# First MLP of a two-layer trunk: up-projection operands formed from unnormalised h, each token's factor applied at the relu, and seven products for all sixteen up quads

## The chip, the cores and the metric

The kernel runs on one core of a Trainium2 chip. The time is that of one execution on the device, in microseconds (us), from several runs; the lower the better. One more execution was taken with the hardware profiler, and all rows below are from it. Engines: PE is TensorE (matmuls; PEld is its weight load), DVE is VectorE, ACT is ScalarE, POOL is GpSimd, and SP issues most of the DMAs.

## The reference, cut to what matters

A trunk of two layers on 1024 tokens of width 1024, all in float32. Layer 0 mixes tokens with a gated MLP, layer 1 with dilated attention. A dense MLP with a squared relu stands behind each mixer. The change touches the MLP of layer 0 and the last projection of the mixer ahead of it.

```
def _rms_norm(x, g):
    y = xf * lax.rsqrt(jnp.mean(xf * xf, axis=-1, keepdims=True) + EPS)
    return (y * g).astype(x.dtype)

for layer in range(DEPTH):                      # DEPTH = 2
    y = _rms_norm(h, mix_norm_g[layer])
    y = mixer(y)                                # layer 0: ... (u * gate) @ w_out
    h = h + y
    y = _rms_norm(h, mlp_norm_g[layer])
    h = h + jnp.square(jax.nn.relu(y @ w_up[layer])) @ w_down[layer]   # 1024 -> 4096 -> 1024
return _rms_norm(h, final_norm_g)
```

The factor of the root mean square is one positive number per token, so relu((r * z) @ w) = r * relu(z @ w), with z = h * g and r the token's factor.

## The kernel before, in words

**Layout.** h is kept transposed: eight tiles `h[m]` of 128 channels by 1024 tokens, worked on in two halves of 512 tokens, s = 0 and 1. A tile of tokens by channels that PE is to use is split in two by `split` (L226, L227): ACT writes the high part in the short float32 format that PE takes in one pass, DVE subtracts it from the source to get the low part. One product of a 128x128 weight block with a block of 128x512 is then three matmuls (high x high, high x low, low x high), issued in L198.

**Products.** The MLP's hidden width is cut in 16 quads. A quad is a 2 x 2 block product: two blocks of 128 hidden channels (i) by two token halves (s), over two halves of the input channels (j), each of 4 tiles. Done plainly that is eight block products of 12 matmuls; with Strassen-like sums of weights and operands it is seven. The seven operands of the tokens' side are called t1 to t7, each of four tiles; t1, t2 and t3 are plain blocks, t4 to t7 are differences. The seven on the weights' side are made by `Weights.steps` from four raw tiles (L382, L383, L384, L387 on GpSimd, splits on ACT and DVE), in the order 4, 1, 5, 6, 2, 7, 3, and they are used in the order 1, 5, 6, 2, 7, 3, 4. Each has a buffer of a pool of eight (`wpool`), which also holds the projection's weights.

**The projection ahead of the MLP.** The groups of output tiles are (0, 1), (2,), (3,), (4, 5, 6, 7), each for both halves. Per tile and half PE does 24 matmuls, `add_h` (L339, DVE) adds the result to h, and `Square.add` squares it on ACT (L279), and adds the squares up on GpSimd (L284), for the last tile on DVE (L288).

**Between projection and MLP.** Behind the last tile of a half, `start_terms` puts a generator on the planner `Flow`. It sums the squares with one-column matmuls, forms the inverse root (`rsqrt`, L256 to L265), spreads it over the partitions by transposes (L205), multiplies h by it (L425 for half 0, L444 for half 1), splits the product, and forms differences (L448, L449 on DVE, L450 and L451 on GpSimd). `Flow` counts the time that PE's instructions take, and lets such a generator go on when its own delay is over; that fixes PE's order at build time. The other engines' orders are made by a list scheduler that goes by program order; `tc.high_priority(offset=PRIO)` moves an instruction 60 places ahead in it. Every engine then works through its queue in order.

**The first two quads.** The differences aren't there yet when the MLP begins, so quads 0 and 1 are done together and plainly, 8 products each, with weights from `plain`: first all of half 0 in four banks, then all of half 1. Relu and square are on ACT (L849, L850), `hidden_terms` forms the operands of the down-projection (L855 to L861). Quads 2 to 4 take seven products through `opening`, which leaves time for the rest of the operands; quads 5 to 15 take the shorter path at the end of `mlp`, in which ACT copies one partial sum from bank to bank (L979) and the results are finished with adds on DVE (L1002, L1008). The second layer's MLP uses the same function.

**Pools.** `slots` has 37 buffers of one 4 KB row per partition (h, the projection's inputs `us`, the operands), `tpool` 13 buffers of half that size.

Of the kernel before, what the change touches and what calls it, by code (L numbers as in the profile page):

```python
# [19 lines left out]
P = 128  # L20
# [11 lines left out]
def half(s):  # L32
    return slice(s * HALF, (s + 1) * HALF)


def blk(b, n=1):
    return slice(b * P, (b + n) * P)
# [72 lines left out]
OPEN = 5  # L110
# [19 lines left out]
def trunk(ctx: ExitStack, tc: tile.TileContext, xT, w_u, w_v, w_o, w_s, b_s, w_qkv, w_vt, w_bo, rel,  # L130
# [63 lines left out]
    def at_bank():  # L194
        return psa.tile([P, HALF], F32, tag="at", name="at")
# [141 lines left out]
    def add_h(o, cols, ps):  # L337
        x = h[o][:, cols]
        nc.vector.tensor_tensor(x, x, ps, op=ALU.add)  # L339
# [165 lines left out]
    def start_terms(sq, s, gi, terms):  # L505
        flow.add((terms.second if s else terms.first)(sq, gi), LAT["sum"])


    wd = {(i, p): dram.tile([P, 2, HALF], F32, name=f"wd{i}_{p}", bufs=1) for i in (*sum(PREPARED, BESIDE), APART) for p in SEVEN}

# [307 lines left out]


    sq = [Square(half(0)), Square(half(1))]  # L820
    terms = Terms()
    for tiles in ((0, 1), (2,), (3,), (4, 5, 6, 7)):
        w = [weight(w_o[m]) for m in tiles]
        for s in range(2):
            for i, m in enumerate(tiles):
                b = mm_bank()
                mm(b, w[i], KCOLS, us[s])
                add_h(m, half(s), b)
                sq[s].add(m)
            if tiles[-1] == 7:  # L830
                start_terms(sq[s], s, 1, terms)
                if s == 0:
                    first = [plain(0, q) for q in range(2)]


    hidden = {}
# [7 lines left out]
        for what, t in terms.items():  # L844
            nc.sync.dma_start(hidden_tile(k, what), t)

    def squared(t, src=None):

        nc.scalar.activation(t, t if src is None else src, AF.Relu)  # L849
        nc.scalar.activation(t, t, AF.Square)  # L850

    def hidden_terms(q, c11, c21, c12, c22, t2, store=True):
# [13 lines left out]
    def mlp(layer, x, first, last, stored=None):  # L866


        def up_weights(q):
            return Weights(lambda i, j: w_up[layer, q, i, j])  # L870


        tiles = [(q, i) for q in range(2) for i in range(2)]
        c = {}

        def held_terms(q):
            hidden_terms(q, c[q, 0, 0], c[q, 1, 0], c[q, 0, 1], c[q, 1, 1], c[q, 0, 0])

        for s in range(2):
            banks = [at_bank() if (n < 2) == (s == 1) else mm_bank() for n in range(4)]  # L880
            if s == 0:
                banks = [mm_bank() if n < 3 else at_bank() for n in range(4)]
            order = [(j, k) for j in range(2) for k in range(4)] if s == 0 else [(j, k) for k in range(4) for j in range(2)]
            for n, (j, k) in enumerate(order):
                xs = x.blocks[j, s]
                flow.until(lambda: len(xs) > k)
                for b, (q, i) in zip(banks, tiles):
                    three(b, first[q][i, j], blk(k), xs[k], n == 0, n == 7)
                    flow.pump()
            for b, (q, i) in zip(banks, tiles):  # L890
                c[q, i, s] = temp()
                with tc.high_priority(offset=PRIO):
                    squared(c[q, i, s], b)
                if s and i and q == 0:
                    held_terms(q)
            if s == 0:
                w = up_weights(2)
                for _ in w.steps():
                    pass
        x.rest()  # L900

        def opening(q, w, more):

            a = mm_bank()
            product(a, w[1], x.t[1])
            if q > 2:
                more()
            u = temp()
            evacuated = nc.scalar.activation(u, a, AF.Copy).ins
            if q == 2:  # L910
                with tc.issue_after(evacuated):
                    more()
# [12 lines left out]
            if q > 2:  # L925
                more()
            nc.vector.tensor_tensor(u, u, b, op=ALU.add)
            e = at_bank()
            product(e, w[7], x.t[7])
            if q > 2:  # L930
                more()
            emptied = nc.vector.tensor_tensor(c22, c22, e, op=ALU.add).ins
            if q == 2:
                with tc.issue_after(evacuated), tc.issue_after(emptied):
                    t4()
                    more()
                    more()
                    held_terms(1)
            nc.vector.tensor_tensor(c22, c22, u, op=ALU.add)
# [12 lines left out]
            nc.vector.tensor_tensor(c21, u, e, op=ALU.add)  # L952
            squared(c21)
            return c11, c21, c12, c22

        for q in range(2, 16):
            down = Down(layer) if q == 15 else None
            wn = down.weights(0) if down else up_weights(q + 1)
            forward, calls = ahead(wn), [0]

            def more():
                forward()
                calls[0] += 1
                if q >= OPEN and calls[0] in LATER:
                    save()
                    next(coming_late[layer], None)
                if q == 15 and calls[0] == 7:
                    save()

            more()  # L970
            if q < OPEN:
                c11, c21, c12, c22 = opening(q, w, more)
            else:
                a = at_bank()
                product(a, w[1], x.t[1])
                more()
# [12 lines left out]
                product(sums, w[6], x.t[6], True)  # L989
                more()  # L990
                c12 = temp()
                with tc.high_priority(offset=PRIO):
                    nc.scalar.activation(c12, sums, AF.Copy)
                if down:
                    down.early(SEVEN[:4])
                product(a, w[2], x.t[2], True)
                more()
                c11 = temp()
                squared(c11, a)
                product(sums, w[7], x.t[7], True)  # L1000
                more()
                nc.vector.tensor_tensor(c22, c22, sums, op=ALU.add)  # L1002
                squared(c22)
                if down:
                    down.early(SEVEN[4:])
                product(d, w[3], x.t[3], True)
                more()
                nc.vector.tensor_tensor(c12, c12, d, op=ALU.add)  # L1008
# [12 lines left out]
        down.close(last, stored)  # L1021
# [935 lines left out]
```

## Time and profile before

| | us |
|---|---|
| median of 3 runs (lowest, highest) | 2108.82 (2108.45, 2113.14) |
| profiled execution | 2107.84 |
| its span, first to last instruction | 2106.1 |
| PE busy | 2083.1 |
| DVE busy | 1572.8 |
| ACT busy | 1183.3 |
| POOL busy | 498.7 |
| mean granted PE clock | 0.998 |

Busy times are shares of the span; a busy PE need not be at its peak, since matmuls overlap. In the rows of the profile "L198 PE MATMUL at<-y,wp" names line, engine, operation, output and inputs; a bracket at the end says how long the engine was idle before and what ended the wait; "x12" is a count.

### The profile page before, as it was taken

How to read it: one execution, taken by the hardware profiler on the slowest of the kernel's cores; microseconds unless marked ns; L12 is line 12 of the kernel's file. 1: busy time of each engine (PE TensorE's matmuls, PEld its weight loads, DVE VectorE, ACT ScalarE, POOL GpSimd, SP SyncE). 2: the span in 40 equal slices, each digit the busy share in tenths (PEclk: the TensorE clock that was granted, in tenths of full speed). 3: DMA queues.
4: the chain of work that ended last, by engine and by line, in shares of the span. 5: the costliest groups of instructions: out<-in, count | busy, mean ns of one | idle time of the engine just before them, and what ended most of it. 6: DMA issues, size and time to landing. Idle time of an engine off the chain costs nothing.

```text
span 2106.1 us, 30736 instructions
## 1 busy us (share of the span) xinstructions
PE 2083.1 (99%) x10160; PEld 1720.9 (82%) x10160; DVE 1572.8 (75%) x2902; ACT 1183.3 (56%) x2387; POOL 498.7 (24%) x368
## 2 busy tenths in 40 slices
PE   9999999999999999999999999999999999999998
PEld 7888888888888888888888788888888888888887
DVE  7878759766689998887746666757985446987776
ACT  7645435566675555435556666776556556544432
POOL 3000124323324333430000000002432222433244
PEclk9999999999999999999999999999999999999999
DMA  6428813688766767644865656482256443655432
GB/s 221 130 91 297 308 36 135 200 278 271 261 221 195 230 213 226 233 160 151 307 208 154 184 163 187 156 271 80 91 196 204 146 152 131 203 163 163 141 115 80
DMA packets 224756, 387.10 MB, mean 184 GB/s; under 512 B 39897, under 2 KB 67668, under 8 KB 224596
## 3 DMA queue, kind: packets, MB, share of 16 engines
q1 hardware_dynamic: 215456, 383.77, 55.4%
q10 hardware_dynamic: 9140, 1.36, 0.4%
q8 instruction: 80, 1.31, 0.3%
q14 instruction: 80, 0.66, 0.1%
HBM read 252.24 MB, written 132.81 MB: 183 GB/s over the span
## 4 chain that ended last, share of the span: by engine, by line
PE 84%; DVE 8%; DMA 2%; ACT 2%; issue 2%; POOL 1%; SPq 0%; DVEq 0%; POOLq 0%; ACTq 0%
PE mm L198 42%; PE at L198 40%; PE at L205 2%; DVE y L227 1%; DVE t L227 1%; DVE tr L227 1%; DMA t<-in_w_qkv 1%; DMA h<-in_xT 1%; DVE wp L227 0%; DVE q L1438 0%; DVE r L444 0%; DVE hx L227 0%; DMA r<-in_w_v 0%; POOL t L284 0%; DVE b L449 0%
## 5 line engine op out<-in xcount | busy, mean ns | idle before, releaser
L227 DVE TENSOR_TENSOR wp<-r,wp 128x512 fp32r<-128x512 f32 (+3 forms) x399 | 324.7, 819 | 124.4 <-ACT wp L226 122.1
L226 ACT ACTIVATE wp<-r 128x512 fp32r<-128x512 f32 (+3 forms) x399 | 236.2, 597 | 317.2 <-PE at L198 195.4
L198 PE MATMUL mm<-t,wp 128*128 128x512 f32 x1368 | 344.8, 395 | 0.0
L198 PE MATMUL at<-hx,wp 128*128 128x512 f32 x1452 | 341.0, 389 | 1.7 <-DVE h L1080 1.6
L198 PEld LDWEIGHTS at<-hx,wp 128*128 128x128 f32 x1452 | 272.1, 188 | 60.0 <-DVE h L1080 3.1
L198 PEld LDWEIGHTS mm<-t,wp 128*128 128x128 f32 x1368 | 250.7, 188 | 52.9 <-issue 0.7
L284 POOL TENSOR_TENSOR t<-t 128x512 f32<-128x512 f32 (+1 forms) x60 | 76.8, 1281 | 801.7 <-ACT t L279 799.7
L198 PE MATMUL at<-y,wp 128*128 128x512 f32 x1008 | 245.3, 389 | 0.0
L198 PE MATMUL mm<-hx,wp 128*128 128x512 f32 x984 | 234.3, 389 | 0.0
L198 PEld LDWEIGHTS at<-y,wp 128*128 128x128 f32 x1008 | 189.0, 188 | 39.6 <-issue 0.4
L198 PEld LDWEIGHTS mm<-hx,wp 128*128 128x128 f32 x984 | 184.5, 188 | 38.7 <-DVE hx L227 0.2
L198 PE MATMUL mm<-y,wp 128*128 128x512 f32 x816 | 209.8, 396 | 1.1 <-DVE y L227 0.6
L382 POOL TENSOR_TENSOR t<-r 128x512 f32<-128x512 f32 (+3 forms) x62 | 85.0, 1372 | 476.3 <-DMA r<-in_w_up 146.4
L198 PEld LDWEIGHTS mm<-y,wp 128*128 128x128 f32 x816 | 149.2, 188 | 33.0 <-DVE y L227 1.1
L227 DVE TENSOR_TENSOR hx<-t,hx 128x512 fp32r<-128x512 f32 x192 | 158.7, 831 | 6.1 <-ACT hx L226 5.6
L198 PE MATMUL mm<-y,whi 128*128 128x512 f32 x512 | 158.3, 390 | 1.1 <-DVE t L790 1.1
L198 PE MATMUL at<-t,wp 128*128 128x512 f32 x552 | 130.6, 389 | 0.0
L226 ACT ACTIVATE hx<-t 128x512 fp32r<-128x512 f32 x192 | 119.1, 628 | 19.9 <-DMA t<-hid 16.0
L384 POOL TENSOR_TENSOR r<-r 128x512 f32<-128x512 f32 (+3 forms) x62 | 90.5, 1459 | 165.4 <-DVE wp L227 151.9
L198 PEld LDWEIGHTS at<-t,wp 128*128 128x128 f32 x552 | 103.6, 188 | 21.5
L1080 DVE TENSOR_TENSOR h<-h,at 128x512 f32<-128x512 f32 x144 | 97.8, 680 | 27.6 <-PE at L198 27.1
L198 PEld LDWEIGHTS mm<-y,whi 128*128 128x128 f32 x512 | 95.5, 188 | 21.1 <-issue 1.5
(247 smaller groups left out, 3466.2 us busy)
## 6 DMA issues: line engine op xcount, KB each, us to landing
t<-hid SPq DMA_DIRECT2D x182, 256.0 KB, 4.3
wd<-tr SPq DMA_DIRECT2D x154, 256.0 KB, 3.1
wp<-wd SPq DMA_DIRECT2D x77, 512.0 KB, 4.2
hid<-t SPq DMA_DIRECT2D x140, 256.0 KB, 2.9
r<-in_w_up SPq DMA_DIRECT2D x120, 256.0 KB, 2.8
r<-in_w_dn SPq DMA_DIRECT2D x80, 256.0 KB, 2.7
hid<-b SPq DMA_DIRECT2D x56, 256.0 KB, 2.9
r<-in_w_v SPq DMA_DIRECT2D x48, 256.0 KB, 3.2
```

Source lines behind the costliest of these rows:

```text
L198: nc.tensor.matmul(out, lhsT, rhs, **kw)
L205: nc.tensor.transpose(out, src, ident)
L226: return (nc.scalar.activation(hi, src, AF.Copy).ins, (engine or nc.vector).tensor_tensor(lo, src, hi.bitcast(F32), op=ALU.subtract).ins)
L227: (engine or nc.vector).tensor_tensor(lo, src, hi.bitcast(F32), op=ALU.subtract).ins)
L284: nc.gpsimd.tensor_tensor(self.acc, self.acc, sq, op=ALU.add)
L382: tt(r3, r[0, 0], r[1, 0], op=ALU.subtract)
L384: tt(r[1, 1], r[1, 0], r[0, 0], op=ALU.subtract)
L1080: return engine.tensor_tensor(hs[i, s], hs[i, s], src, op=ALU.add).ins
```

## The change

A new class `RawTerms` takes the place of `Terms` for the first MLP. As each projected tile leaves PE, its operands are made from h times the channel's weight only (`put`): from half 0 t1 (m = 0 to 3) and t2 (m = 4 to 7); from half 1 t5 (m = 0 to 3), and for m = 4 to 7 t7, t6, t3 and t4 together. The inverse root is still formed per half (`norm`), but it is only copied to an SBUF row tile (`rows`), and multiplied in at the relu, which moves from ACT to one DVE instruction (maximum with 0, times the row). `add_h` of the projection gets priority. All sixteen quads of the first MLP then take seven products on the shorter path, starting with quad 0; the weights of quad 0 come from `Weights` in place of `plain`. The second MLP keeps its path.

```
+    class RawTerms:
+        def __init__(self, gi):
+            self.t = {p: [] for p in range(1, 8)}
+            self.g = vec[:, gi, :]
+            self.neg = ...                         # -g
+            self.rows = slot(name="rows")
+        def scaled(self, p, x, g):
+            hi, lo = pair(f"t{p}").both()
+            nc.scalar.activation(hi, x, AF.Copy, scale=g)
+            nc.vector.scalar_tensor_tensor(lo, x, g, hi.bitcast(F32), op0=ALU.mult, op1=ALU.subtract)
+            self.t[p].append(Pair((hi, lo)))
+        def put(self, m, s):
+            j, k = divmod(m, 4)
+            stt = nc.vector.scalar_tensor_tensor
+            x0, x1 = h[m][:, half(0)], h[m][:, half(1)]
+            g = self.g[:, m:m + 1]
+            if s == 0:
+                self.scaled(1 + j, x0, g)
+            elif j == 0:
+                t5 = temp()
+                nc.scalar.activation(t5, x1, AF.Copy, scale=g)
+                stt(t5, x0, self.neg[:, m:m + 1], t5, op0=ALU.mult, op1=ALU.add)
+                self.t[5].append(pair("t5").split(t5))
+            else:
+                g0, y, t = self.g[:, k:k + 1], temp(), temp()
+                nc.scalar.activation(y, h[k][:, half(1)], AF.Copy, scale=g0)
+                stt(t, x1, g, y, op0=ALU.mult, op1=ALU.subtract)
+                t7 = pair("t7").split(t)
+                stt(y, h[k][:, half(0)], g0, t, op0=ALU.mult, op1=ALU.add)
+                self.t[6].append(pair("t6").split(y))
+                self.t[7].append(t7)
+                self.scaled(3, x1, g)
+                stt(t, x0, g, y, op0=ALU.mult, op1=ALU.subtract)
+                self.t[4].append(pair("t4").split(t))
+        def norm(self, sq, s):
+            yield from sq.sums()
+            r = sq.rms()
+            yield LAT["rms"]
+            pb = spread(r)
+            with tc.high_priority(offset=PRIO):
+                nc.scalar.activation(self.rows[:, half(s)], pb, AF.Copy)
...
-    terms = Terms()
+    terms = RawTerms(1)
...
                 mm(b, w[i], KCOLS, us[s])
-                add_h(m, half(s), b)
+                with tc.high_priority(offset=PRIO):
+                    add_h(m, half(s), b)
                 sq[s].add(m)
+                terms.put(m, s)
             if tiles[-1] == 7:
-                start_terms(sq[s], s, 1, terms)
+                flow.add(terms.norm(sq[s], s), LAT["sum"])
                 if s == 0:
-                    first = [plain(0, q) for q in range(2)]
+                    first = Weights(lambda i, j: w_up[0, 0, i, j])
+                    for _ in first.steps():
+                        pass
...
-    def squared(t, src=None):
-        nc.scalar.activation(t, t if src is None else src, AF.Relu)
+    def squared(t, src=None, rows=None):
+        src = t if src is None else src
+        if rows is None:
+            nc.scalar.activation(t, src, AF.Relu)
+        else:
+            nc.vector.scalar_tensor_tensor(t, src, 0.0, rows, op0=ALU.max, op1=ALU.mult)
         nc.scalar.activation(t, t, AF.Square)
...
+        begin = 0 if rows[0] is not None else 2     # the plain start only where begin is 2
...
-        for q in range(2, 16):
+        for q in range(begin, 16):
...
-            if q < OPEN:
+            if begin and q < OPEN:
                 c11, c21, c12, c22 = opening(q, w, more)
...
-                squared(c11, a)
+                squared(c11, a, rows[0])
...
-                squared(c22)
+                squared(c22, None, rows[1])
...
-                squared(c12)
+                squared(c12, None, rows[1])
...
-                squared(c21, sums)
+                squared(c21, sums, rows[0])
```

More of the change, by code (lines that the diff above doesn't have):

```diff
@@ L506, in start_terms @@
         flow.add((terms.second if s else terms.first)(sq, gi), LAT["sum"])
+    class RawTerms:
+        def __init__(self, gi):
+            self.t = {p: [] for p in range(1, 8)}
+            self.g = vec[:, gi, :]
+            self.neg = small.tile([P, KT], F32, name="neg", bufs=1)
+            nc.vector.tensor_scalar(self.neg, self.g, -1.0, None, op0=ALU.mult)
+            self.rows = slot(name="rows")
[34 more added lines that the diff above has]
+                nc.scalar.activation(self.rows[:, half(s)], pb, AF.Copy)
     wd = {(i, p): dram.tile([P, 2, HALF], F32, name=f"wd{i}_{p}", bufs=1) for i in (*sum(PREPARED, BESIDE), APART) for p in SEVEN}
@@ L870, in up_weights @@
             return Weights(lambda i, j: w_up[layer, q, i, j])
[L873 to L886, printed above, removed]
-                for b, (q, i) in zip(banks, tiles):
[L888 to L899, printed above, removed]
@@ L900, in mlp, with held_terms @@
-        x.rest()
+        rows = [x.rows[:, half(s)] for s in range(2)] if isinstance(x, RawTerms) else [None, None]
+        begin = 0 if rows[0] is not None else 2
+        w = first
+        if begin:
+            tiles = [(q, i) for q in range(2) for i in range(2)]
+            c = {}
+            def held_terms(q):
+                hidden_terms(q, c[q, 0, 0], c[q, 1, 0], c[q, 0, 1], c[q, 1, 1], c[q, 0, 0])
+            for s in range(2):
+                banks = [at_bank() if (n < 2) == (s == 1) else mm_bank() for n in range(4)]
+                if s == 0:
+                    banks = [mm_bank() if n < 3 else at_bank() for n in range(4)]
+                order = [(j, k) for j in range(2) for k in range(4)] if s == 0 else [(j, k) for k in range(4) for j in range(2)]
+                for n, (j, k) in enumerate(order):
+                    xs = x.blocks[j, s]
+                    flow.until(lambda: len(xs) > k)
+                    for b, (q, i) in zip(banks, tiles):
+                        three(b, first[q][i, j], blk(k), xs[k], n == 0, n == 7)
+                        flow.pump()
+                for b, (q, i) in zip(banks, tiles):
+                    c[q, i, s] = temp()
+                    with tc.high_priority(offset=PRIO):
+                        squared(c[q, i, s], b)
+                    if s and i and q == 0:
+                        held_terms(q)
+                if s == 0:
+                    w = up_weights(2)
+                    for _ in w.steps():
+                        pass
+            x.rest()
```

## Prediction

> **What bounds the kernel now.** I read the totals and the chain first, then the work by stage, then the matmul, vector and GpSimd streams between the last output-projection tile and up quad 2, where the diff lies.
>
> ```profile
> span 2106.1 us, 30736 instructions
> PE 2083.1 (99%) x10160; PEld 1720.9 (82%) x10160; DVE 1572.8 (75%) x2902; ACT 1183.3 (56%) x2387; POOL 498.7 (24%) x368
> PE 84%; DVE 8%; DMA 2%; ACT 2%; issue 2%; POOL 1%; SPq 0%; DVEq 0%; POOLq 0%; ACTq 0%
> ```
>
> TensorE is busy for 99% and carries the chain: 23 us are idle in all. So a matmul taken out is time gained, and any wait put in front of TensorE is time lost. DVE at 75% has room on the average only, so the stages decide (columns: stretch, length, busy time and instructions of PE, PEld, DVE, ACT, POOL, clock, DMA share, GB/s).
>
> ```profile
> 222.00:263.00 41.00, 41.00 (x183) 33.95 (x182) 29.82 (x46) 17.94 (x33) 8.47 (x6) 1.00 0.86 300
> 263.00:284.00 21.00, 20.84 (x98) 17.08 (x97) 5.64 (x13) 5.80 (x10) 4.12 (x4) 1.00 0.13 41
> 284.00:305.00 21.00, 21.00 (x100) 17.52 (x99) 17.48 (x32) 10.37 (x18) 4.25 (x3) 1.00 0.15 51
> 312.00:330.00 18.00, 17.55 (x78) 14.20 (x77) 17.56 (x23) 11.17 (x20) 9.53 (x6) 1.00 0.20 76
> 350.00:368.00 18.00, 18.00 (x81) 14.91 (x80) 17.90 (x22) 10.93 (x21) 10.26 (x7) 1.00 0.70 244
> 440.00:480.00 40.00, 40.00 (x177) 32.04 (x176) 25.78 (x36) 24.81 (x44) 12.37 (x9) 1.00 0.77 266
> ```
>
> The last group of projection tiles (m = 4 to 7, column half 0, then half 1) ends at 299.2. DVE is already full from 312 to 368, where the terms of the second half and their differences are made. Yet PE loses almost nothing there, because eight plain products for each of two quads run while DVE catches up:
>
> ```profile
> 299.21 2.20 PE L198 MATMUL mm<-y,wp 128*128 128x512 f32 x9
> 302.61 0.95 PE L198 MATMUL at<-ones,t 128*128 128x1 f32 x8
> 303.42 1.65 PE L198 MATMUL mm<-y,wp 128*128 128x512 f32 x6
> 306.96 0.60 PE L205 MATMUL at<-ident,rq 128*128 128x128 f32 x4
> 307.31 0.94 PE L198 MATMUL mm<-y,wp 128*128 128x512 f32 x3
> 324.36 1.65 PE L198 MATMUL mm<-y,wp 128*128 128x512 f32 x6 [0.45 <-ACT t L849]
> 343.55 4.24 PE L198 MATMUL mm<-y,wp 128*128 128x512 f32 x18
> 410.35 2.72 PE at L198 x12
> ```
>
> Twelve matmuls, one product, take 2.72 us, 0.2267 each. The first up matmul starts at 299.21. Six of the eighteen at 343.55 still belong to quads 0 and 1, so quad 2 begins at 343.55 + 1.36 = 344.91: 45.70 us for the two quads. Of these 192 x 0.2267 = 43.5 are matmuls; the rest is the eight sum-of-squares matmuls (302.61 to 303.42), the four transposes (306.96 to 307.31) and 0.45 of waiting.
>
> **The change, part by part.**
>
> (1) *Products.* Quads 0 and 1 go from 16 to 14 products: 24 matmuls, -5.44 us. Without new waits the stretch is 168 x 0.2267 + 0.81 + 0.35 = 39.2 us against 45.70: -6.5. The 0.45 wait goes because the four banks that were emptied together are no longer used.
>
> (2) *Vector work moves ahead of its cover.* Before, the second half's terms were needed only from 322 on. Now all seven operands are made from h as the tiles leave PE. The durations:
>
> ```profile
> 282.21 0.69 DVE L339 TENSOR_TENSOR h<-h,mm 128x512 f32<-128x512 f32 x1 [1.47 <-PE mm L198]
> 291.42 2.06 DVE L425 SCALAR_TENSOR_TENSOR keep<-h,vec,at 128x512 f32<-128x512 f32 x3
> 299.51 0.68 DVE L339 TENSOR_TENSOR h<-h,mm 128x512 f32<-128x512 f32 x1
> 300.11 1.29 DVE L227 TENSOR_TENSOR wp<-r,wp 128x512 fp32r<-128x512 f32 x2
> 301.31 0.69 DVE L288 TENSOR_TENSOR t<-t 128x512 f32<-128x512 f32 x1
> 303.88 0.16 DVE L258 TENSOR_SCALAR rv<-at 128x4 f32<-128x4 f32 x1 [1.88 <-ACT sd L256]
> ```
>
> Back to back, a two-input operation comes every 0.60 us (1.29 for two) and a scalar one every 0.66 (2.06 for three). In half 1 each of m = 4 to 7 now asks DVE for four scalar operations (t, y, the low part of t3, t4) and three low parts: 4 x 0.66 + 3 x 0.60 = 4.44 us, plus add_h 0.60, against 5.44 of PE per tile. In that stretch fall also the seven weight splits of quad 0, whose buffers come free with the same tiles. The squares' total of half 1 (L288, at 301.31 before) keeps its plain priority, so it stands in DVE's queue behind all that m = 4, 5 and 6 left. From add_h of m = 4 (282.21) to the end of that total: 4 add_h, 7 splits, 3 x 7 for the operands less the one whose high part comes later, the total itself, and five small steps of half 0: 20 x 0.60 + 12 x 0.66 + 0.8 = 20.7, done at 302.9. PE wants it at 302.61, as before, after 15 matmuls of the new product stream. So on bare durations it is about in time (wait 0.3), with nothing in hand: whatever slows DVE in these 20 us is a PE wait of the same size.
>
> (3) *GpSimd slows it.* In the stretch lie seven GpSimd operations of 128x512: the square sums of m = 4, 5, 6, two for quad 0's weights (the two others can run earlier), two for quad 1's. What one costs DVE:
>
> ```profile
> 316.83 1.60 POOL L450 TENSOR_TENSOR keep<-r 128x512 f32<-128x512 f32 x1 [2.56 <-DVE b L448]
> 316.60 0.68 DVE L227 TENSOR_TENSOR y<-r,y 128x512 fp32r<-128x512 f32 x1
> 317.20 1.78 DVE L449 TENSOR_TENSOR b<-r,b 128x512 f32<-128x512 f32 x1
> ```
>
> L449 took 1.78 instead of 0.68: +1.10, until GpSimd had ended. Averages lie lower: 312 to 330 holds 23 DVE operations, at 0.62 each 14.2 of 17.56, so 3.4 over six GpSimd operations, 0.56 each; 350 to 368 gives 17.90 - 22 x 0.60 = 4.7 over seven, 0.67. There a good part of DVE's work reads PSUM; in the new stretch only the add_h do. I take 0.85, between 0.67 and 1.10: 7 x 0.85 = 6.0. Ends: 5 x 0.56 = 2.8 (quad 1's two too late to count) and 7 x 1.10 = 7.7. With the 0.3: **a wait of 6.3 us** (3.1 to 8.0), ahead of the sum-of-squares matmuls in quad 0's second product. It replaces the missing cover, and gives DVE time to finish t6, t7, t3, t4 of m = 7, which are wanted later.
>
> [...]
>
> (4) *The clock after such a wait.* The longest PE gap in the trace is at the very end:
>
> ```profile
> 2093.68 1.95 PE L198 MATMUL at<-ones,t 128*128 128x1 f32 x16 [0.30 <-POOL t L284]
> 2097.98 0.66 PE L205 MATMUL at<-ident,rq 128*128 128x128 f32 x2 [2.35 <-DVE rq L265]
> 2094.00:2096.00 2.00, 1.63 (x15) 1.54 (x14) 1.68 (x5) 0.95 (x4) 0.00 (x0) 1.00 0.51 197
> 2096.00:2098.00 2.00, 0.02 (x1) 0.06 (x1) 2.00 (x9) 0.00 (x0) 0.00 (x0) 0.81 0.72 265
> 2098.00:2100.00 2.00, 0.64 (x2) 0.23 (x2) 2.00 (x6) 1.18 (x3) 0.47 (x1) 0.50 0.88 330
> 1.12 4.50 PE L223 MATMUL idle<-ones 128*128 128x128 f32 x22 [1.12 <-DVE scalars L216]
> ```
>
> PE stops at 2095.63; the granted clock averages 0.81 over the next 2 us and is 0.50 after. So a gap of six us very probably halves it. The recovery isn't in this trace. At the start PE works 4.4 us on small matmuls before the real ones, which bounds it: 0 to 4.4 us at half speed, 0 to 2.2 lost. I take 1.4, above the middle, since the gap is long.
>
> [...]
>
> (5) *Smaller edits.* Four relus per quad go from ACT (0.633 each) to DVE: 2.7 to 4.4 us per quad of 19.04. At 440 to 480 DVE has 25.78 of 40, so 31 to 35 after: no wait. One point could fail: PE's last product of a quad overwrites the bank that c22's add reads.
>
> ```profile
> L849 ACT ACTIVATE t<-t 128x512 f32<-128x512 f32 x62 | 39.2, 633 | 23.7 <-DVE t L939 10.2 <-DVE t L952 9.4 <-DVE t L1002 0.8
> 454.58 0.69 DVE L1002 TENSOR_TENSOR t<-t,mm 128x512 f32<-128x512 f32 x1 [0.36 <-PE mm L198]
> 457.30 0.69 DVE L1008 TENSOR_TENSOR t<-t,at 128x512 f32<-128x512 f32 x1 [1.36 <-PE at L198]
> ```
>
> DVE waits for PE there, and one product (2.72) less the add leaves 2.0 in hand: 0, without cover up to 2 us in quad 0. From 222 to 263 twelve operations (7.6) come to DVE's 29.82 of 41, and 263 to 284 (5.64 of 21) takes what is left over; weights and banks have a tile or more in hand. add_h gets priority: 0. ACT gains five operations per tile of half 1 and stays under 75%. Before, 16 scalings, 16 splits and their differences stood on DVE after 284, and eight differences on GpSimd; they go, and eight weight combinations for quads 0 and 1 come to GpSimd, four of them counted in (3). Loads and SP's queue: eight raw tiles before, eight after, nothing queued behind. The 37 slots are just filled; the operands of m = 6 and 7 use those of us[1], freed inside the last tile: 0 to 0.5.
>
> **Sum**, against the profiled execution (2107.84 us, 1.7 outside its span): 39.2 + 6.3 + 1.4 = 46.9 against 45.70, +1.2. The median shown is 2108.82, 0.98 higher; the forecast is 2108.82 + 1.2 = **2110.0 us**. Its own range: 39.2 + 3.1 + 0 = 42.3 (-3.4) to 39.2 + 8.0 + 2.2 = 49.4 (+3.7), with (5) up to +6: 2105.4 to 2114.8.
>
> **Rivals.**
> *A, the wait doesn't come.* If GpSimd's operations fall where DVE waits for ACT anyway, or the total is queued sooner, (3) and (4) vanish: -6.5 + 0.3 = -6.2, 2102.6. For it: in 284 to 305 three GpSimd operations ran beside a DVE at 17.48 of 21 without a stretched one. Against: those DVE operations mostly read PSUM. Chance 0.19, a little over half of that with a gain over 0.3%, since the bound lies at 2102.5.
> *B, slower.* Quad 0's c22 add stands behind DVE's backlog, and PE stops a second time before the last product, just after the first stop. It decides when more than 2.0 us of DVE work are ahead of that add. Price: 2 us for the stop, 2.2 for the clock a second time, first wait at its upper end 8.0 + 2.2: 39.2 + 14.4 = 53.6, +7.9, 2116.7. For it: DVE ran full from 312 to 368 before too. Against: the first stop lets DVE catch up. Chance 0.15.
> *C, no real saving.* Relus on DVE make every quad late by 0.5: +8 us over 16 quads, net +9, 2118. Against: 31 to 35 of 40. Chance 0.06.
>
> **How the numbers follow.** The main case has 0.60. A measurement here tells about 0.3% (6.3 us) from no change. Faster: 0.12 from A, 0.01 from the main case's edge. Slower: B and C nearly whole, 0.19. Same: 0.68. For 8 in 10 the range goes from inside A to B: 2103.0 to 2116.5.
>
> **What would show it.** Right: two quads in 14 products; one PE gap of 3 to 8 us before the one-column matmuls, released by the DVE add of the squares; DVE full from 283 to about 315, low parts near 1.8 beside GpSimd; clock below 1.00 after the gap; no PE waits in quads 1 to 15. Wrong: no such gap (A), a second gap before a product that rewrites a bank (B), a short gap in every quad (C).

## The result, and the profile after

The changed kernel takes 2123.89 us (median of 4 runs, 2119.36 to 2128.06) against 2108.68 for the kernel before (four runs, one more than in the table above): a ratio of 1.0069, 95% interval 1.0057 to 1.0080. It is 15.2 us slower. The forecast was 2110.0, with a range up to 2116.5; the measured time lies above it. The profiled execution took 2123.02 us. Its totals:

```profile
span 2121.3 us, 30753 instructions
PE 2084.1 (98%) x10136; PEld 1718.3 (81%) x10136; DVE 1625.3 (77%) x2956; ACT 1158.9 (55%) x2344; POOL 497.2 (23%) x367
```

The 24 matmuls are gone (10160 to 10136), but PE's busy time didn't fall and the span grew by 15.2. Part of the matmuls must have run more slowly, and PE must have idled. The matmul stream of the first quads shows where (start, length, what ran, count, in brackets the idle time before it and its releaser):

```profile
299.90 3.56 PE L198 MATMUL at<-t,wp 128*128 128x512 f32 x15
311.81 1.87 PE L198 MATMUL at<-ones,t 128*128 128x1 f32 x8 [8.35 <-DVE t L288]
313.54 4.19 PE L198 MATMUL at<-t,wp 128*128 128x512 f32 x9
317.53 2.35 PE L198 MATMUL mm<-t,wp 128*128 128x512 f32 x6
319.72 0.60 PE L205 MATMUL at<-ident,rq 128*128 128x128 f32 x4
351.47 0.84 PE L198 MATMUL at<-t,wp 128*128 128x512 f32 x3
625.52 0.84 PE L198 MATMUL mm<-hx,wp 128*128 128x512 f32 x3
```

Up begins at 299.90 (before: 299.21). After fifteen matmuls PE stands still for 8.35 us, until the DVE addition that totals half 1's squares (L288) is done. Then the eight one-column and fifteen full matmuls from 311.81 to 319.72 take 7.91 us, where 0.81 + 15 x 0.2267 = 4.2 would do. The clock of that time, by stretches (length; busy time of PE, PEld, DVE, ACT, POOL; granted clock):

```profile
303.00:305.00 2.00, 0.46 (x3) 0.04 (x1) 2.00 (x2) 0.58 (x1) 1.92 (x2) 1.00 0.00 0
305.00:307.00 2.00, 0.00 (x0) 0.00 (x0) 2.00 (x3) 0.90 (x3) 0.52 (x1) 0.65 0.00 0
307.00:319.00 12.00, 7.19 (x21) 6.03 (x22) 9.10 (x19) 6.68 (x14) 1.71 (x1) 0.50 0.07 23
319.00:321.00 2.00, 2.00 (x12) 1.63 (x11) 1.49 (x3) 1.74 (x4) 0.00 (x0) 0.94 0.00 0
440.00:480.00 40.00, 40.00 (x176) 32.15 (x174) 33.20 (x44) 20.60 (x37) 12.89 (x8) 1.00 0.83 274
```

PE works at half speed from 311.81 to about 319.2: 3.7 us more. (Below, the clock at half is called cold, at full speed warm.) Quad 2 begins at 351.47, so quads 0 and 1 take 51.57 us instead of 45.70. Why the total came late is seen on DVE and GpSimd:

```profile
300.86 1.78 DVE L521 SCALAR_TENSOR_TENSOR t<-h,vec,t 128x512 fp32r<-128x512 f32 x1
302.57 1.82 DVE L545 SCALAR_TENSOR_TENSOR t<-h,vec,t 128x512 f32<-128x512 f32 x1
304.31 1.75 DVE L539 SCALAR_TENSOR_TENSOR t<-h,vec,t 128x512 f32<-128x512 f32 x1
306.59 0.74 DVE L541 SCALAR_TENSOR_TENSOR t<-h,vec,t 128x512 f32<-128x512 f32 x1
311.07 0.69 DVE L288 TENSOR_TENSOR t<-t 128x512 f32<-128x512 f32 x1
300.66 1.45 POOL L284 TENSOR_TENSOR t<-t 128x512 f32<-128x512 f32 x1 [4.05 <-ACT t L279]
302.56 1.29 POOL L382 TENSOR_TENSOR t<-r 128x512 f32<-128x512 f32 x1 [0.46 <-DMA r<-in_w_up]
303.92 1.60 POOL L383 TENSOR_TENSOR r<-r 128x512 f32<-128x512 f32 x1
```

DVE works without a break; an operation that took 0.74 by itself (306.59) took 1.75 to 1.82 beside each of the GpSimd operations shown. From the addition to h of m = 4 (282.91) to the end of the total (311.76) seven DVE operations are stretched so, beside seven GpSimd operations, by 0.60 to 1.10 each and 6.7 us together.

The second loss was put at nothing in the forecast. From quad 2 (351.47) to the first down matmul (625.52) pass 274.05 us; before, 344.91 to 613.46, 268.55. First PE's waits in that stretch (line waited for, total, times, longest), then the place of the longest on DVE, PE and SP's DMA queue:

```profile
PE mm L198 <- DVE t L1062: 2.3, 1, 2.3
PE mm L198 <- ACT t L1053: 1.3, 3, 0.7
```

```profile
602.28 0.69 DVE L653 TENSOR_TENSOR tr<-tr 128x512 f32<-128x512 f32 x1 [1.58 <-DMA tr<-in_w_qkv]
602.89 0.68 DVE L1062 TENSOR_TENSOR t<-t,mm 128x512 f32<-128x512 f32 x1
603.63 3.02 PE L198 MATMUL mm<-t,wp 128*128 128x512 f32 x12 [2.26 <-DVE t L1062]
596.29 3.01 SPq L187 DMA_DIRECT2D r<-in_w_dn  x2
599.35 0.42 SPq L187 DMA_DIRECT2D tr<-in_w_qkv  x1
```

c22's addition (L1062), which empties the bank that PE's next product rewrites, stands in DVE's queue behind L653. That one prepares weights for later and waits for a load, which SP issued only at 599.35. So DVE was late for PE here although it had itself idled for 1.58 us. The two rows of waits hold 3.6 of the 5.5 us; the rest stands in no row of this view. The account: 0.7 later start + 5.9 in quads 0 and 1 + 5.5 in quads 2 to 15 + 3.1 from the first down matmul to the end (1495.8 against 1492.6) = 15.2.

### The profile page after: what moved, and what is told of

The parts are those of the page before. It is cut to its first block, busy times and chain, and to the rows that moved or that the text cites. A ratio compares the mean times of both kernels' runs of the same rounds, so it can differ in the third digit from the quotient of the medians.

```text
span 2121.3 us, 30753 instructions
## 1 busy us (share of the span) xinstructions
PE 2084.1 (98%) x10136; PEld 1718.3 (81%) x10136; DVE 1625.3 (77%) x2956; ACT 1158.9 (55%) x2344; POOL 497.2 (23%) x367
## 3 DMA queue, kind: packets, MB, share of 16 engines
q8 instruction: 80, 1.31, 0.2%
## 4 chain that ended last, share of the span: by engine, by line
PE 65%; DVE 7%; DMA 2%; issue 2%; ACT 2%; POOL 1%; SPq 0%; DVEq 0%; POOLq 0%; ACTq 0%
PE mm L198 32%; PE at L198 31%; PE at L205 2%; DVE wp L227 1%; DMA r<-in_w_dn 1%; DVE t L227 1%; POOL t L284 1%; DVE y L227 1%; DVE hx L227 0%; DMA t<-hid_(0, 0)_6200 0%; DVE h L339 0%; DMA r<-in_w_vt 0%; DVE h L1140 0%; DVE q L1498 0%; DMA tr<-in_w_qkv 0%
## 5 line engine op out<-in xcount | busy, mean ns | idle before, releaser
L227 DVE TENSOR_TENSOR wp<-r,wp 128x512 fp32r<-128x512 f32 (+3 forms) x403 | 329.2, 822 | 96.9 <-ACT wp L226 94.6
L198 PE MATMUL mm<-t,wp 128*128 128x512 f32 x1548 | 390.1, 396 | 3.7 <-DVE t L1062 2.3
L198 PEld LDWEIGHTS mm<-t,wp 128*128 128x128 f32 x1548 | 284.5, 188 | 66.2 <-ACT t L1053 3.8
L198 PE MATMUL at<-t,wp 128*128 128x512 f32 x1044 | 249.4, 391 | 0.0
L198 PEld LDWEIGHTS at<-t,wp 128*128 128x128 f32 x1044 | 197.0, 189 | 41.3 <-issue 0.4
L198 PE MATMUL mm<-y,wp 128*128 128x512 f32 x624 | 162.3, 398 | 0.8 <-DVE y L227 0.6
L384 POOL TENSOR_TENSOR r<-r 128x512 f32<-128x512 f32 (+3 forms) x64 | 94.8, 1482 | 179.0 <-DVE wp L227 155.6
L198 PEld LDWEIGHTS mm<-y,wp 128*128 128x128 f32 x624 | 113.3, 188 | 25.1 <-DVE y L227 1.0
L198 PE MATMUL at<-y,wp 128*128 128x512 f32 x504 | 122.6, 389 | 0.0
L906 ACT ACTIVATE t<-t 128x512 f32<-128x512 f32 x128 | 80.2, 631 | 72.9 <-DVE t L905 70.5
```

The lines of the kernel that those rows point to most:

```text
L198: nc.tensor.matmul(out, lhsT, rhs, **kw)
L227: (engine or nc.vector).tensor_tensor(lo, src, hi.bitcast(F32), op=ALU.subtract).ins)
L384: tt(r[1, 1], r[1, 0], r[0, 0], op=ALU.subtract)
```

## The experiments

The main questions: is it GpSimd that delays the total; is the order of DVE's queue at fault; are the relus the cause in the later quads; and can a rearranged kernel keep the gain. Each is compared with the kernel before, run beside it.

**Is it the place in the queue or the amount of work?** The square of tile 7 and its total get priority:

```
-                sq[s].add(m)
+                with tc.high_priority(offset=400) if (m, s) == (7, 1) else nullcontext():
+                    sq[s].add(m)
```

> The changed kernel, with the square and the squares' total of the last tile (m = 7, half 1) moved as far ahead in priority as the scheduler lets them. Theory 'amount' (DVE simply has more to do than fits before 303, because GpSimd stretches it): the total can overtake only two operations, 1.4 us, so PE's gap shrinks from 8.35 to about 7, the clock still falls, and the time stays 12 to 15 us above the kernel before. Rival 'place' (the total only stands badly in the queue): the gap falls below 2 us, the clock stays at 1.00, and the time drops by about 10 us, to 3 to 6 above the kernel before.

Measured: 2124.66, ratio 1.0071 (1.0053 to 1.0088), as slow as without.

```profile
311.01 1.87 PE L198 MATMUL at<-ones,t 128*128 128x1 f32 x8 [6.98 <-DVE t L288]
```

The gap shrank by 1.4 us, since the total overtook only two operations. The later quads took that back: the wait for c22's addition is 3.25 us against 2.26, and the clock falls behind it (0.61 at 605 to 607, 0.53 at 607 to 609), where it stayed at 1.00 in the changed kernel. So the place in the queue was not the matter.

**Is it GpSimd?** GpSimd's weight combinations of quads 0 and 1 and three of its additions of squares are left out, the seven operations of the stretch among them:

```
+        if self.alone:            # weights of quads 0 and 1: split only, not combined
+            ... self.split(p, src[p]) ...
+            return
+    elif k in self.left_out:      # squares of m = 4, 5, 6 of half 1
+        pass
```

> The changed kernel without the GpSimd work beside the critical stretch: the weight combinations of quads 0 and 1 of the first MLP are left out (raw weights are split in their place), and so are the additions of the squares of m = 4, 5, 6 in half 1; all DVE and ACT work stays. Theory 'GpSimd stretches DVE' (seven operations at 1.1 each): the gap before the squares' total shrinks from 8.35 to 0.3 to 1.5 us, the clock stays at 1.00, and quad 2 begins 10 to 12 us earlier than in the changed kernel; the time is 2 to 5 above the kernel before (the later loss of about 5.5 in quads 2 to 15 stays). Rival 'DVE's own work or its waits for ACT are too long': gap of 6 us or more, time 12 to 15 above.

Measured: 2117.42, ratio 1.0035 (1.0024 to 1.0046).

```profile
305.68 1.05 PE L198 MATMUL at<-ones,t 128*128 128x1 f32 x8 [1.84 <-DVE t L291]
```

```profile
307.00:309.00 2.00, 2.00 (x7) 1.57 (x6) 1.66 (x6) 0.56 (x2) 0.00 (x0) 0.53 0.00 0
309.00:311.00 2.00, 2.00 (x7) 1.57 (x6) 1.42 (x5) 0.57 (x2) 0.00 (x0) 0.62 0.00 0
```

The gap falls from 8.35 to 1.84: 6.5 us of it were GpSimd's, 0.93 for each of the seven, which fits the 6.7 us of stretched operations. What is left of the gap has another cause:

```profile
293.37 0.75 DVE L553 SCALAR_TENSOR_TENSOR t<-h,vec,t 128x512 f32<-128x512 f32 x1 [1.37 <-ACT t L552]
```

DVE stood idle for 1.37 us until ACT had scaled a tile (1.31 us at the same place in the changed kernel). And behind the gap of 1.84 us the clock was at half for some 3.4 us (means of 0.53 and 0.62 in two stretches of 2 us). The waits of the later quads stay and grow (3.4 us for c22's addition, 1.4 for c12's copy). ACT's copy in quad 2 stands 46.2 us behind up's first matmul, 54.6 in the changed kernel: 8.4 us won there, of which the quads behind give 2.6 back (325.62 us from first up to first down matmul, 319.8 here): 1.1 in the longer wait for c22's addition, and most of the rest by the clock, which falls behind that wait (0.57 at 597 to 601).

**Are the relus the cause in quads 1 to 15?** The relus go back to ACT, without the factor:

```
-        rows = [x.rows[:, half(s)] for s in range(2)] if isinstance(x, RawTerms) else [None, None]
+        rows = [None, None]
```

> The changed kernel with the relus back on ACT in all sixteen quads; the tokens' factor is left out there. Theory 'relus on DVE cost the 5.5 us of quads 2 to 15' (the hidden tiles come later, their stores hold up SP's queue, the loads behind them land late, and an add or copy that PE waits for stands behind the instruction that waits for the load): these waits (2.26, 0.71, 0.28, 0.27) go, quads 2 to 15 lose no more than the 2 us of the kernel before, the gap of 8.35 before them stays; time 8 to 11 above the kernel before. Rival 'the shift of the stage or the shorter path itself': waits and loss stay, time 13 to 16 above.

Measured: 2118.51, ratio 1.0037 (1.0024 to 1.0050). ACT's copy at L1039 (L979 before) comes once in every quad; eleven of them, from quad 5 to quad 15, pace the quads of the three kernels. Before, changed, and with the relus on ACT:

```profile
L979 ACT ACTIVATE mm<-at x11: 580/582/582, 405.0 to 597.4; 128x512 f32<-128x512 f32 x11
```

```profile
L1039 ACT ACTIVATE mm<-at x11: 578/582/582, 411.6 to 610.0; 128x512 f32<-128x512 f32 x11
```

```profile
L1039 ACT ACTIVATE mm<-at x11: 582/582/587, 412.9 to 605.4; 128x512 f32<-128x512 f32 x11
```

```profile
313.96 1.87 PE L198 MATMUL at<-ones,t 128*128 128x1 f32 x8 [8.25 <-DVE t L288]
```

Ten quads take 192.4 us before, 198.4 changed, and 192.5 with the relus on ACT, while the gap in quad 0 stays at 8.25. From quad 2 to the first down matmul pass 268.52 us with the relus on ACT, 268.55 before. So the relus' move to DVE is the whole cause of the later quads' loss, and the gap in quad 0 doesn't hang on it.

**Is the cold clock a loss of its own?** 36 extra matmuls keep PE busy in the gap:

```
+            if s:
+                x, ps = self.t[1][0], at_bank()
+                for i in range(36):
+                    nc.tensor.matmul(ps, x.hi[:, 0:P], x.hi, start=i == 0, stop=i == 35)
             yield from sq.sums()
```

> The changed kernel with 36 extra matmuls of 128x512 (8.2 us, result unused) on PE in front of the squares' total of half 1, in the place of the gap. Theory 'the gap costs a second time through the clock': clock 1.00 throughout, the 8.35 us gap becomes at most 0.5, matmuls behind it come at 0.227 at once, and the stretch is 3.7 us shorter: 10.5 to 12.5 above the kernel before. Rival 'the matmuls behind the gap are slow because their operands come late': no gain, 14 to 16 above.

Measured: 2131.23, ratio 1.0095 (1.0077 to 1.0113), a miss.

```profile
313.85 1.02 PE L198 MATMUL at<-ones,t 128*128 128x1 f32 x8 [0.28 <-DVE t L288]
322.86 1.09 PE L205 MATMUL at<-ident,rq 128*128 128x128 f32 x4 [4.43 <-DVE rq L265]
319.83 0.63 ACT L226 ACTIVATE t<-t 128x512 fp32r<-128x512 f32 x1 [2.91 <-DVE t L545]
320.36 0.25 ACT L256 ACTIVATE sd<-at,scalars 128x4 f32<-128x4 f32 x1
```

```profile
323.00:325.00 2.00, 2.00 (x7) 1.74 (x8) 0.31 (x1) 0.60 (x1) 0.00 (x0) 0.50 0.15 49
```

PE stayed warm through the first gap (granted clock 1.00 from 311 to 321) and reached the four transposes early, but waited 4.43 us there for the tokens' factor (L265); then the clock fell all the same (0.69 at 321 to 323). The factor was late because its square root (L256) stood on ACT behind a split that waited 2.91 us for DVE: it began 5.5 us after the one-column matmuls had ended (314.87). In the changed kernel it began at 313.72, at once behind them, and the factor was done at 316.71, 3.0 us before the transposes. So this run changed the order on ACT as well, and doesn't show whether the 3.7 us could be had back.

**Can the work be ordered better?** First another order of the projection's tiles, so that the pairs of the differences come earlier; then t3 and t4 of tiles 4 to 7 held back until the total is issued:

```
-    for tiles in ((0, 1), (2,), (3,), (4, 5, 6, 7)):
+    for tiles in ((0, 4), (1,), (5,), (2, 6, 3, 7)):
```

> The changed kernel with the projection's tiles in the order (0, 4), (1,), (5,), (2, 6, 3, 7), so that two of the four heavy operand sets (t7, t6, t3, t4) are made a stage earlier. Theory 'amount in front of the squares' total': six us of DVE work leave the stretch (two sets of 4.44 become two of 1.26 for t5), the gap of 8.35 falls to 1 to 3 us, what the clock takes falls with it to 0 to 2; quads 2 to 15 still lose their 5.5: 5 to 9 us above the kernel before. Rival 'the work only moves': the earlier stage (DVE 30 of 41 us before) is overfull then, PE waits there for weights or sums, and the total stays 12 us or more above.

```
+                def rest():                       # t3 and t4 of m = 4..7
+                    self.scaled(3, x1, g)
+                    ...
+    with tc.issue_after(sq[1].added):
+        for rest in terms.later: rest()
```

> The changed kernel with t3 and t4 of m = 4 to 7 held behind the squares' total on DVE. They are first wanted 13.6 us after the MLP begins. Theory 'amount in front of the total': eight DVE operations, 5.2 us, leave the queue ahead of it, and the gap falls from 8.35 to 2 to 3.5 us; the clock still drops for some us (a gap of 1.84 was enough in the run without GpSimd work); 6 to 10 us above the kernel before. Rival 'the same wait at the next place': PE then stands at t6, t7, t3 or t4 for as long, 13 us or more above.

Measured: 2124.27 for the order, ratio 1.0072 (1.0057 to 1.0087), a miss; 2119.44 for the deferral, ratio 1.0049 (1.0033 to 1.0066), with the gap as expected and the time just above what was expected. PE's gaps, the order first:

```profile
283.71 1.86 PE L198 MATMUL at<-ones,t 128*128 128x1 f32 x8 [3.35 <-DVE t L288]
313.34 1.05 PE L198 MATMUL at<-ones,t 128*128 128x1 f32 x8 [3.02 <-DVE t L288]
```

```profile
307.15 1.56 PE L198 MATMUL at<-ones,t 128*128 128x1 f32 x8 [3.02 <-DVE t L288]
```

With the new order half 0's total is late as well (3.35 us, and a cold clock behind it: the eight one-column matmuls take 1.86 us, 0.95 in the kernel before), and up begins at 306.76 instead of 299.90: the backlog was only moved ahead. The deferral holds back two scalar operations and a split for each of four tiles. Six of these scalar operations and two of the splits stood ahead of the total in the changed kernel, 6 x 0.66 + 2 x 0.60 = 5.2 us of DVE, and the gap falls by 5.3 us.

**The factor applied elsewhere.** h is divided by the squared factor during up and multiplied by it at the end of down, so that the relus can be on ACT; then the same with the order and a deferral of m = 6, 7:

```
+            nc.vector.reciprocal(v, self.rows[:, half(s)])
+            for m in range(KT):
+                nc.vector.tensor_tensor(x, x, v, op=ALU.mult)     # x: h[m], half s
...
+                        nc.vector.tensor_tensor(x, x, terms.rows[:, cols], op=ALU.mult)   # after down
```

> The changed kernel with relus on ACT and the tokens' factor taken out of the quads: h is divided by its square during the up-projection (16 multiplications and two reciprocals on DVE) and multiplied by it again behind the last down-projection product (16 multiplications). The whole reference is computed. Theory 'the relus on DVE cost quads 2 to 15 their 5.5 us': as in the run with relus on ACT, those waits go, the gap of 8.35 stays, and 0 to 2 us come back for the multiplications at the end: 8 to 11 us above the kernel before. Rival 'any 32 operations cost as much': 13 us or more above.

> The tile order of c1, t3 and t4 of m = 6 and 7 held back as in c2, and the factor taken out of the quads as in c3. The whole reference is computed. If both causes are the whole story, the gap before the squares' total is under 1 us with the clock at 1.00, quads 2 to 15 lose no more than the kernel before (2 us), and the 24 matmuls saved show: 6 us below to 1 us above the kernel before. If the pieces trade places, a new wait of several us stands somewhere between 222 and 320: 3 to 8 above.

Measured: 2149.30, ratio 1.0193 (1.0178 to 1.0208), and 2145.08, ratio 1.0168 (1.0153 to 1.0183); both far from expected. Of the first:

```profile
322.69 3.34 DVE L556 RECIPROCAL rowv<-rows 128x512 f32<-128x512 f32 x1
341.76 0.63 ACT L226 ACTIVATE t<-t 128x512 fp32r<-128x512 f32 x1 [8.11 <-DVE h L560]
342.44 1.95 PE L198 MATMUL mm<-t,wp 128*128 128x512 f32 x3 [8.89 <-ACT t L226]
```

```profile
925.00:970.00 45.00, 35.94 (x134) 27.76 (x133) 39.21 (x59) 13.55 (x24) 19.25 (x14) 0.84 0.42 146
```

The quads run at 19.04 again (three at 19.69, as before, and the last at 20.72), but the multiplications of h crowd DVE's queue between 327 and 342, seven of them in a row from 337.43, and PE waited 8.89 us for an operand behind them. The multiplications at the end stand in the open behind down: from 925 to 970 PE works 35.94 of 45 us, at a clock of 0.84.

**Both causes taken out.** The edits of the GpSimd and the ACT experiments together:

> Both suspected causes are taken out together: the relus of the first MLP are on ACT with the tokens' factor left out of them, and GpSimd's weight combinations of quads 0 and 1 and its additions of the squares of tiles 4 to 6 of half 1 are left out (so that hidden values and factors are not the reference's). Alone, the first took 5.4 us from the changed kernel's median and the second 6.5. If they are two separate causes, the sum is some 12 us: about 8.1 to 8.5 above minus 5 to 6 of them, that is 2111 to 2113, 2 to 5 above the kernel before. Theory 'same cause seen twice' (DVE short of time, and either edit relieves all of it): about 2117, no better than the better one alone. From the first matmul of up to that of down: 313 to 314 us by the first (325.62 - 6.34 - 5.8), 319 by the second. What would still stand against the 2102 of a change without any stall is the clock after the gap of some 2 us, and 2 to 3 us behind the first MLP.

Measured: 2107.65, ratio 0.9994 (0.9984 to 1.0003), below the 2111 to 2113 that was expected.

```profile
306.18 1.05 PE L198 MATMUL at<-ones,t 128*128 128x1 f32 x8 [1.82 <-DVE t L291]
312.21 0.60 PE L205 MATMUL at<-ident,rq 128*128 128x128 f32 x4
```

```profile
309.00:311.00 2.00, 2.00 (x6) 1.51 (x6) 1.92 (x5) 0.24 (x1) 0.00 (x0) 0.50 0.00 0
```

```profile
343.96 1.30 PE L198 MATMUL at<-t,wp 128*128 128x512 f32 x5
612.48 0.84 PE L198 MATMUL mm<-hx,wp 128*128 128x512 f32 x3
```

16.2 us below the changed kernel, more than the 11.9 of the two alone: two separate causes. Some 2.6 of the 4.3 us between are what the later quads gave back in the run without GpSimd's work; they don't here (268.52 us from quad 2 to the first down matmul). The rest was not traced. Up's first matmul is at 300.80 and quad 2 begins at 343.96, so quads 0 and 1 take 43.16 us: 39.2 + 1.82 of gap + 1.8 of cold clock (306.18 to 312.21 is 6.0 us for matmuls of 4.2), with 0.3 over. So the products did save their 6.5 us, to 0.3. Yet the kernel is no faster than the one before: of the 2.5 us that quads 0 and 1 gain on it, 1.6 go since up begins later (300.80 against 299.21), and 0.6 behind the first down matmul.

**Moving the load waits, and the best order found.** The points at which a quad prepares later weights are moved away from c22's addition and c12's copy; then this with t7's splits behind the last square, t3 and t4 behind the factor, and the squares of m = 5, 6, 7 summed on PE alone; then the deferral and the squares on PE, without the moved points, with the relus on ACT and the factor left out of them:

```
-                if q >= OPEN and calls[0] in LATER:
+                if q >= OPEN and calls[0] in (LATER if begin else (3, 5, 7)):
...
-    sq = [Square(half(0)), Square(half(1))]
+    sq = [Square(half(0)), Square(half(1), (0, 5, 6))]
+                self.later[0].append(lambda: self.t[7].append(pair("t7").split(t)))
+                self.later[1].append(lambda: self.scaled(3, x1, g))
+                self.later[2].append(fourth)      # t4
```

> Only the calls at which the quads of the first MLP prepare the later weights are moved, from the 2nd, 4th and 6th point of a quad to the 3rd, 5th and 7th: the weight preparation's instructions then no longer stand right ahead of c22's addition and c12's copy, for which the PE waits. Nothing is left out. Theory 'place' (the relu made the DVE queue longer, and what hurts is that c22's addition and c12's copy stand behind an instruction that waits for a weight load): the waits of 2.26, 0.71 and 0.28 us go, quads 7 to 15 come near 19.04 and 19.7 us each, 3 to 5 us are won, 2119 to 2121. Theory 'amount' (the DVE has too much to do in a quad with the relus): the PE waits elsewhere in the quad, the sum of the excess over 19.04 stays at 4 to 6 us, 2123 to 2125.

> Nothing is left out; three moves together. The weight preparation goes to the 3rd, 5th and 7th point of a quad; the splits of t7 of all tiles stand behind the square of tile 7, and t3 and t4 behind the second factor; the squares of tiles 5, 6 and 7 of half 1 go to the PE's column sums one by one, without additions on GpSimd and DVE. In the run that held back t3 and t4 of the tiles 4 to 7 behind the total, the gap was 3.02 us and the time 2119.4. Here 2.8 us of DVE (four splits of 0.69) and the last addition (0.6) leave the way to the total as well, and one more GpSimd addition beside it: a gap of 0 to 1 us, the clock stays near 1.00, quad 0 begins at 300 and quad 1 at 319 to 321: about 2111 if the quads keep their loss of 5 us, 2107 if moving the weight preparation takes most of it. Rival: t3 or t4 come late for the products 3 and 4 of quad 0, a new wait of 3 to 5 us there, and 2113 to 2117.

> The deferral of t7, t3 and t4 and the squares summed on the PE as in the kernel beside it, the weight preparation where it was, and the relus of the first MLP on ACT with the tokens' factor left out of them. If the gap in quad 0 and the relus on DVE are the whole of the loss, this gives what the seven products were to bring: 2103 to 2107, from first up to first down matmul 307 to 310 us. If something else takes 3 us or more, 2108 to 2112.

Measured: 2121.18, ratio 1.0058 (1.0043 to 1.0074); 2117.15, ratio 1.0043 (1.0029 to 1.0058); 2112.32, ratio 1.0015 (1.0005 to 1.0024). With the points moved, two waits are left:

```profile
542.18 3.04 PE L198 MATMUL mm<-t,wp 128*128 128x512 f32 x12 [0.92 <-DVE t L1062]
601.75 3.02 PE L198 MATMUL mm<-t,wp 128*128 128x512 f32 x12 [1.64 <-DVE t L1062]
```

Fifteen of ACT's copies span 273.2 us there, 274.3 in the changed kernel and 268.6 with the relus on ACT. So moving these points won only 1.1 of 5.7 us; the rest stays as long as the relus are on DVE. That it hangs on the amount of DVE work in a quad is likely but not shown, and through which waits it comes stays open. In the best order the first gap is gone, and the next thing is late:

```profile
318.65 0.57 ACT L1065 ACTIVATE t<-mm 128x512 f32<-128x512 f32 x1
319.27 4.62 PE L198 MATMUL mm<-t,wp 128*128 128x512 f32 x12 [2.81 <-ACT t L1065]
```

c12's copy stood on ACT behind the deferred splits; the clock fell to 0.58 after it (319 to 321). That is the rival of its expectation by another instruction. The last run has a gap of the same length for the same copy (2.81 us, until 320.36). So it missed the 2103 to 2107 that were expected, although its later quads lose almost nothing (269.29 us from quad 2 to the first down matmul). No version that leaves nothing out beats the kernel before; the best is 8.5 us behind.

## Why the prediction was wrong

(1) *Products*, -6.5 us: right. With both causes out, quads 0 and 1 account for it to 0.3.

(2) *DVE in time on bare durations, wait 0.3*: too small. Without GpSimd's operations the wait was 1.84. The count of DVE work ahead of the total was right, 20 two-input and 12 scalar operations; what it put at nothing was a wait of DVE itself, 1.37 us for ACT (1.31 in the changed kernel). With it the sum closes: 20.7 + 6.7 of stretching + 1.3 = 28.7 us, against 28.85 from 282.91 to 311.76.

(3) *GpSimd adds 6.0*: right, 6.5 measured. The wait as a whole, 8.35, lies just above the upper end of 8.0, because of (2). A single operation took 1.78 beside GpSimd (300.86) and 0.74 alone, but seven GpSimd operations cost 0.93 each, less than their own 1.29 to 1.74: the DVE operation at 302.57 ended 0.54 us after the GpSimd operation that it began with, and alone it takes 0.75 (310.41), so by this count some 0.2 us of its own time passed beside GpSimd's. The prediction took the averages of the kernel before as too low for this stretch, since much of DVE's work there reads PSUM; its row at 291.42 agrees: three operations that read PSUM took 2.06 us together, unstretched, with a GpSimd operation beside them from 291.71 to 293.00.

(4) *The clock, 1.4*: 3.7 measured, above the bound of 2.2. The bound came from the start of the program, 4.4 us of small matmuls, which in the kernel before took 0.42 us each at first and 0.27 at the end (some 3.8 us at half speed); here PE worked for about 7.4 us before the clock came back, the first 1.7 of them on one-column matmuls. In the run with both causes out, where the gap was 1.82, the loss was 1.8.

(5) *Relus on DVE at nothing*: this is the step that failed. The load came out as forecast: 33.20 of 40 us at 440 to 480, against 31 to 35. The conclusion "no wait" did not follow. DVE, 83% busy, working in order, and itself waiting for loads and for ACT, came late for PE in most quads from the fifth on, by up to 2.1 us (the spacing of ACT's copies, against that with the relus on ACT). That is rival C's mechanism, with 5.7 us between the copies of quads 1 and 15 instead of 8 over all sixteen; it had been given 0.06.

(6) From down's first matmul to the end the changed kernel takes 3.1 us more, which the forecast had at nothing. Of these, 2.1 lie ahead of PE's last two transposes (at 2112.11, before at 2097.98) and 1.1 behind them. With both causes out it takes 0.6 more. The cause was not traced to an instruction.

The sum was 39.2 + 6.3 + 1.4 = 46.9; measured is 39.2 + 8.35 + 3.7 + 0.3 = 51.57, then 5.5 in the quads, 3.1 behind them and 0.7 ahead. Of the miss of 14.0 us, 4.7 lie in quads 0 and 1, in the terms (2) to (4); 5.5 are (5), 3.1 are (6), and 0.7 is up's later start.

## What to carry to other kernels

A busy share of 80% on an engine that works in order is no proof of "no wait" (here DVE was 83% busy, and PE waited up to 2.3 us for it): look at what stands right ahead of the instruction that PE waits for, and at whether that one can wait for a load or another engine. When work is moved to an earlier stage, count all of it up to the instruction that PE wants first, with the slowdown by GpSimd (0.93 us for each of its operations here) and with that engine's own waits, and bound the price of a gap with its cold clock by more than the gap (8.35 + 3.7 us and 1.82 + 1.8 us here). When one wait is taken away, look for the next one behind it before counting the gain: in the best order above it was ACT's copy.

## What was not expected of the hardware

After a PE gap of 1.84 us the granted clock was at half for some 3.4 us (0.53 and 0.62 in the two stretches after 307), with the eight one-column matmuls right behind the gap. It was still 1.00 up to 307, 3.2 us after the end of the last full matmul (303.84). The run with the extra matmuls has a gap in quad 14 with full matmuls on both sides, and the clock falls behind it too (0.73 at 611 to 613, 0.50 at 613 to 615):

```profile
611.58 4.61 PE L198 MATMUL mm<-t,wp 128*128 128x512 f32 x12 [2.03 <-DVE t L1066]
```

In the changed kernel the longer gap of 2.26 us at the same place (603.63, with 3.02 us for the twelve matmuls behind it) left the clock at 1.00. So in these runs the clock fell without the one-column matmuls too, and the length of the gap alone doesn't decide. After the gap of 8.35 us the clock was at half for about 7.4 us of PE work, where the prediction had taken at most 4.4. The time at half clock behind a gap, worked out from the windows of these runs, is 3.4 us behind the 1.84 without GpSimd's work, behind the 1.82 with both causes out, and behind the 2.81 of the best order and of the last run; 6.8 behind the wait of 4.43 in the run with the extra matmuls; 10.2 behind the 8.25 with the relus on ACT; and 13.7 in the changed kernel (305.6 to 319.3). In the changed kernel PE worked for 7.4 us of these 13.7, nine full matmuls from 313.54 to 317.53 came every 0.44 us in place of 0.2267, and 3.7 us were lost.
